# A pair's two heads on the row halves of the array in the scans' scores, and a later unpacking of the inverted triangles

## The chip, the core and the metric

The kernel runs on one core of a Trainium2 chip. The metric is the device time of one execution in microseconds. Three runs of the kernel before took 4954.92 to 4966.74 us, with a median of 4965.7 us.

## What is computed

Two layers over 2048 latent tokens and 256 context tokens of width 1024. The second layer is attention of a differential kind and isn't touched. The first is an RWKV-7 mixer: for each of 16 heads of size 64 a state S of 64 x 64 is carried over the tokens, once forward and once backward.

```python
def step(S, inp):
    r_t, w_t, k_t, v_t, kk_t, a_t = inp
    sa = jnp.einsum("bhvk,bhk->bhv", S, kk_t)
    S = (S * w_t[:, :, None, :]
         - sa[..., None] * (kk_t * a_t)[:, :, None, :]
         + v_t[..., None] * k_t[:, :, None, :])
    return S, jnp.einsum("bhvk,bhk->bhv", S, r_t)
...
oc_f, sc_f = scan_direction(con, 0, s0, False)
oc_b, sc_b = scan_direction(con, 1, s0, True)
ol_f, _ = scan_direction(lat, 0, sc_f, False)
ol_b, _ = scan_direction(lat, 1, sc_b, True)
```

The kernel works in chunks of 64 tokens. Within a chunk the recurrence becomes matrix products of 64 x 64 for each head (the scores), a triangular inverse for each head, and a short chain that takes the state from chunk to chunk.

## The kernel before, in words

`block` runs `setup`, `phase1` (projections and streams, written to DRAM), `phase2` (the scans), `readout`, `project1`, `attention` and `finish`. The change touches `phase2` alone, which lies at about 1150 to 2270 us of the profiled span.

**The loop.** There are 36 chunks in each direction, taken alternately: step q works on direction q % 2. The loop runs over q from -9 to 71. In one pass it makes the scores of step s = q + 9 and the chain of step q, so scores lie nine steps ahead. The order of work on TensorE, VectorE, ScalarE and GpSimd is the order in which the program lists it (`in_order`). SP, which issues all DMAs, isn't in that list: its order is made by the framework's planner.

**One pass.** Each kind of work is a generator that is advanced piece by piece. `step(c)` comes first (L796: the two products with RX, 32 records each for LA and LB), then the pieces in the order of `MAIN`, where u is `unpack`, b is `turned`, g is `scores`, j is `join` and c is `chain`:

```python
MAIN = "ubgjugbcgujgc"
```

So a pass has three slots for u (positions 0, 4 and 9), two for b (four transposes of BK each, L773, copied to KB by ScalarE, L774), four for g, two more for the chain (L804, and then L813 and L818 with the updates of RX and the store of o, L827) and two for j (U by VectorE at L742, and L749 with its copies).

**Scores.** A pair p holds two heads, A on partitions 0 to 63 (LO) and B on 64 to 127 (HI). For head A the tiles are BA and LA, loaded on LO and zero on HI; for head B they are BB and LB, loaded on HI and zero on LO. Each matmul contracts over all 128 rows. The four pieces of g are A with pairs 0 to 3, A with 4 to 7, B with 0 to 3 and B with 4 to 7. A piece takes one PSUM bank of a pool of three (`sc`, shared with `turned`), issues four f32 matmuls of 128 x 128 x 128 (L680, two records each), and then ScalarE copies parts to A32 (L687, twice) and E (L690), and VectorE makes the two masked products, one into the other half of L (L691) and one into Pb (L692).

**Loads.** `load(s)` issues BA, LA, BB and LB (L666, 256 KB each). BA and BB have two buffers, LA and LB ten. The zeros of the other halves are written once by GpSimd (L839).

**Inversion.** When four steps of scores are there (s % 4 == 3, so q % 4 == 2), VectorE transposes A32 to N (L699, L700) at the end of the pass, and GpSimd runs 30 rank-1 steps on it (L701 to L710). Four steps later, in the pass with q % 4 == 2, `unpack` makes four transposes on VectorE: two to Tt (L715, L717) and two to Dg (L719, L721). Three fall in that pass, one at each slot for u, and the fourth at slot 0 of the next. That next pass also has `join_rows` right after `step(c)` (L733, it reads Tt) and `join(0)` (it reads Dg).

Of the kernel before, what the change touches and what calls it, by code (L numbers as in the profile page):

```python
# [11 lines left out]
F32 = mybir.dt.float32  # L12
# [609 lines left out]
def phase2(k):  # L622

    nc, tc, S = k.nc, k.tc, k.S
    ident = k.ident
    LO, HI = slice(0, 64), slice(64, 128)
    LEAD = 9
    with ExitStack() as st:
        pool = lambda name, bufs, **kw: st.enter_context(tc.tile_pool(name=name, bufs=bufs, **kw))
        c0 = pool("p2z", 1)  # L630
# [16 lines left out]
        f2 = lambda ap: ap.rearrange("p a b -> p (a b)")  # L647
        ji = "p i j -> p j i"


        wide = [128, NPAIR, 2, 64]
        space = lambda pool, name: pool.tile(wide, F32, name=name)
        BAs, BBs, LAs, LBs = ([space(c0, f"{name}0")] for name in ("BA", "BB", "LA", "LB"))
        for i in range(1, LEAD + 1):
            for ring, name in ((LAs, "LA"), (LBs, "LB"), (BAs, "BA"), (BBs, "BB")):
                if i == 1 or ring is LAs or ring is LBs:
                    ring.append(space(c2[i - 3] if i > 2 else cb if i == 1 and name[0] == "L" else ca, f"{name}{i}"))
        Dg = c2[-1].tile([128, 32, 32], F32, name="Dg")
        U = c2[-1].tile([128, 32, 64], F32, name="U")

        def load(s):
            d, n = s % 2, ORDER[s % 2][s // 2]
            LA, LB = LAs[s % (LEAD + 1)], LBs[s % (LEAD + 1)]
            BA, BB = BAs[s % 2], BBs[s % 2]
            for t, nm, rows in ((BA, "bk", LO), (LA, "qr", LO), (BB, "bk", HI), (LB, "qr", HI)):
                nc.sync.dma_start(out=t[rows], in_=S[nm][d, n, rows])  # L666
            return LA, LB, BA, BB

        def scores(d, par, loaded, A32, E, Pb):

            LA, LB, BA, BB = loaded
            yield LA, LB, Pb
            br, kr = brow[d], krow[d]
            for ab in range(2):
                L, B = ((LA, BA), (LB, BB))[ab]
                for q in range(2):
                    ps = sc.tile([128, 4, 2, 64], F32, name="scps")
                    for j in range(4):
                        p = 4 * q + j
                        nc.tensor.matmul(f2(ps[:, j]), f2(B[:, p]), f2(L[:, p]), start=(j == 0), stop=True,  # L680
                                         skip_group_check=True)
                    prs = slice(4 * q, 4 * q + 4)
                    h0 = 8 * ab + 4 * q
                    c0 = 16 * par + h0
                    for blk in range(2):
                        r = slice(br.start + 32 * blk, br.start + 32 * blk + 32)
                        nc.scalar.copy(A32[r, :, c0:c0 + 4].rearrange("p t c -> p c t"),  # L687
                                       ps[r, :, d, 32 * blk:32 * blk + 32])
                    e, ec = (slice(0, 32), slice(32, 64)) if d == 0 else (slice(96, 128), slice(0, 32))
                    nc.scalar.copy(E[e, c0:c0 + 4, :], ps[e, :, d, ec])  # L690
                    nc.vector.tensor_tensor(L[krow[ab], prs], ps[kr], bcast(mk[kr, d], 1, 4), op=ALU.mult)  # L691
                    nc.vector.tensor_tensor(Pb[br, h0:h0 + 4], ps[br, :, 1 - d], bcast(mk[br, d, 1 - d], 1, 4),  # L692
                                            op=ALU.mult)
                    yield
# [138 lines left out]
        none = inv = iter(())  # L833
        step = lambda g: next(g, None)
        loaded[0], loaded[1] = load(0), load(1)
        for i in range(LEAD + 1):
            for t, rows in ((BAs, HI), (LAs, HI), (BBs, LO), (LBs, LO)):
                if i < len(t):
                    nc.gpsimd.memset(t[i][rows], 0.0)  # L839
            if i == 0:  # L840
                mk = causal_masks(k, ca)
        RX = []
        for d in range(2):
            RX.append(new_rx(0, d))
# [18 lines left out]
                yield from modulation(k, layer, lo, hi, 2, space, {lo // 4: bank()}, lambda: space()[0:2, :512], bank)  # L863

        at = (nq - LEAD) % (LEAD + 1)
        done = itertools.cycle((BAs[0], BBs[0], LAs[at], LBs[at]))
        free = lambda: next(done).rearrange("p a b c -> p (a b c)")
        mods = [none, none]
        if k.mod:
# [2 lines left out]
        with in_order(k, mybir.EngineType.PE, mybir.EngineType.DVE, mybir.EngineType.Activation, mybir.EngineType.Pool):  # L872
            for q in range(-LEAD, nq):
                s = q + LEAD
                b = c = g = u = j = none
                if 0 <= q + 1 < nq:
                    keys[q + 1] = load_keys(q + 1)
                if q >= 0:
                    KB = kp.tile(wide, F32, name="KB")
                    b = turned(keys.pop(q), KB)  # L880
                    c = chain(q // 2, q % 2, q // 2 % 2, prep.pop(q), KB)
                step(c)
                more = q >= -2 and q - q % 4 + 4 < nq
                if more and q % 4 == 3:
                    for par in range(2):
                        join_rows(tiles[q // 4 + 1][1], par)
                    j, late = join(0), join(1)
                if more and q % 4 == 2:
                    unp = unpack(tiles[q // 4 + 1][2])
                    u = none if q < 0 else unp  # L890
                if more and q % 4 == 3:
                    u = unp
                if q >= 0 and q % 4 == 0:
                    j = late
                if s < nq:
                    if s % 4 == 0:
                        tiles[s // 4] = [ip.tile([128, 32, 32], F32, name="A32", bufs=1),
                                         ip.tile([128, 32, 32], F32, name="E", bufs=2), None]
                    A32, E, _ = tiles[s // 4]
                    if s % 2 == 0:  # L900
                        Pb = pb.tile([128, 16, 64], F32, name="Pb")
                    g = scores(s % 2, s // 2 % 2, loaded.pop(s), A32, E, Pb)
                    prep[s] = step(g)
                who = {"u": u, "j": j, "b": b, "c": c, "g": g}
                for at, name in enumerate(MAIN):
                    step(who[name])
                    if name == "g":
                        step(inv)
                    if s >= nq and at in TAIL:
                        step(mods[1])  # L910
                    if -5 <= q < 0 and at in FILL:
                        step(mods[0])
                if q == -2:
                    for who in (inv, inv, unp, unp, unp):
                        step(who)
                if 1 <= s < nq - 1:
                    loaded[s + 1] = load(s + 1)
                if s < nq and s % 4 == 3:
                    inv = invert(A32, nc.vector if s < 4 else nc.gpsimd)
                    tiles[s // 4][2] = step(inv)  # L920
                    if s >= 4:
                        for _ in inv:
                            pass
# [774 lines left out]
```

## Time and profile before

| | |
|---|---|
| median of three runs | 4965.7 us |
| profiled execution, time | 4953.41 us |
| its span | 4951.7 us |
| TensorE busy | 4658.2 us (94%) |
| VectorE busy | 3706.7 us (75%) |
| ScalarE busy | 2700.0 us (55%) |
| GpSimd busy | 1457.7 us (29%) |
| granted clock, mean | 0.972 |

The shares are means over stages with different limits, so they say little of the scan. The rows that matter are those of the stretch from 1300 to 2100 us, in which the scan runs in a steady state. TensorE's records overlap, so that the start of one group to the start of the next tells more than the busy time. An entry such as `[0.55 <-POOL N L710]` is idle time of that engine just before the instruction, and what ended it.

### The profile page before, as it was taken

Reading aid. Unit: us, or ns where it says so; the run is one execution under the profiler, and the core shown is the slowest. Engines: PE = TensorE matmul, PEld = TensorE weight load, DVE = VectorE, ACT = ScalarE, POOL = GpSimd, SP = SyncE. Lnnn points to the kernel's source line nnn. Section 1 sums busy time; section 2 is a strip of 40 time slices with the busy share of each in tenths; the row PEclk is TensorE's granted clock in tenths of the full one; section 3 lists DMA queues with packets and bytes.
Section 4 is the critical chain, followed back from the end, with each engine's and each line's share of the span. In section 5 each row is a group of like instructions: output and inputs, shape, how many; then the busy total and the mean of one; then the engine's idle time right before and its main releaser. Section 6 shows DMA issues by size and latency. Waiting matters only on the chain.

```text
span 4951.7 us, 100950 instructions
## 1 busy us (share of the span) xinstructions
PE 4658.2 (94%) x40786; PEld 4184.8 (85%) x40786; DVE 3706.7 (75%) x5806; ACT 2700.0 (55%) x4908; POOL 1457.7 (29%) x1806
## 2 busy tenths in 40 slices
PE   7999999997998889888989999989999999999999
PEld 5999999995888888876768888879888888898887
DVE  6888887887877777866768258238989989989843
ACT  4655655554666666655541221227777777777730
POOL 1222112112566565551312022022223323323300
PEclk8999999998999998989999999989999999999999
DMA  4565565557666676668853332230011011010042
GB/s 165 170 185 159 176 187 165 162 165 208 151 163 165 166 177 155 168 182 284 265 173 99 115 115 86 94 105 19 11 46 36 14 42 36 28 29 18 10 158 94
DMA packets 624787, 612.13 MB, mean 124 GB/s; under 512 B 31622, under 2 KB 529721, under 8 KB 623297
## 3 DMA queue, kind: packets, MB, share of 16 engines
q1 hardware_dynamic: 621841, 601.99, 42.1%
q8 instruction: 323, 5.29, 0.5%
q10 hardware_dynamic: 2480, 3.67, 0.2%
q14 instruction: 143, 1.17, 0.1%
HBM read 405.79 MB, written 199.77 MB: 122 GB/s over the span
## 4 chain that ended last, share of the span: by engine, by line
PE 62%; DVE 14%; issue 11%; DMA 5%; ACT 5%; POOL 2%; SPq 0%; ACTq 0%; POOLq 0%; DVEq 0%
PE mmps L939 18%; PE mmps L363 9%; PE pv L1462 8%; PE tps L1455 4%; PE sc L1416 4%; PE sc L1417 3%; PE xops L818 3%; PE scps L680 3%; DVE p L1419 3%; PE xops L796 3%; DVE p L1440 2%; DMA RS<-s_v 2%; PE chps L813 1%; PE tps L1365 1%; DVE U L742 1%
## 5 line engine op out<-in xcount | busy, mean ns | idle before, releaser
L1430 ACT ACTIVATE p<-p,m 128x2304 f32<-128x2304 f32 x256 | 568.8, 2222 | 201.6 <-DVE p L1419 199.4
L1462 PE MATMUL pv<-v,at 128*128 128x128 f32 x4608 | 626.1, 277 | 6.2 <-ACT at L1457 4.4
L1462 PEld LDWEIGHTS pv<-v,at 128*128 128x128 f32 x4608 | 564.3, 191 | 16.0 <-ACT at L1457 12.8
L1416 PE MATMUL sc<-ks,qh 128*128 128x512 f32 (+1 forms) x1280 | 520.1, 406 | 15.2 <-DVE p L1419 15.1
L1417 PE MATMUL sc<-ks,ql 128*128 128x512 f32 (+1 forms) x1280 | 463.9, 372 | 0.3 <-POOL ql L1397 0.3
L363 PE MATMUL mmps<-hH,wH 128*128 128x386 f32 x1632 | 429.5, 343 | 17.1 <-DVE sg L581 12.0
L1457 ACT COPY at<-tps 128x512 f32<-128x512 f32 (+1 forms) x640 | 345.3, 540 | 177.6 <-PE tps L1455 173.6
L363 PE MATMUL mmps<-hL,wH 128*128 128x386 f32 x1632 | 427.2, 342 | 8.4 <-DVE hL L92 8.4
L1440 DVE SCALAR_TENSOR_TENSOR p<-p,r,p 128x1152 f32<-128x1152 f32 x256 | 427.4, 1670 | 4.5
L939 PE MATMUL mmps<-wH,hH 128*128 128x512 f32 x1088 | 424.6, 390 | 3.1 <-ACT hH L91 3.1
L363 PE MATMUL mmps<-hH,wL 128*128 128x386 f32 x1632 | 425.0, 341 | 0.3 <-DVE nm_ss L197 0.3
L939 PE MATMUL mmps<-wH,hL 128*128 128x512 f32 x1088 | 424.0, 390 | 0.7 <-DVE hL L92 0.7
L939 PE MATMUL mmps<-wL,hH 128*128 128x512 f32 x1088 | 424.2, 390 | 0.0
L1419 DVE TENSOR_SCALAR_CACHE_REDUCE p<-sc,m 128x1280 f32<-128x1280 f32 x256 | 395.5, 1545 | 17.1 <-PE sc L1417 1.2
L1397 POOL TENSOR_TENSOR ql<-qt,qh 128x256 fp32r<-128x256 f32 x128 | 112.2, 877 | 977.8 <-ACT qt L1396 916.5
L1455 PE MATMUL tps<-ident,p 128*128 128x128 f32 x2304 | 361.5, 275 | 10.1 <-ACT qt L1396 5.2
L1419 DVE TENSOR_SCALAR_CACHE_REDUCE p<-sc 128x1024 f32<-128x1024 f32 x256 | 311.5, 1217 | 56.7 <-PE sc L1417 55.6
L1455 PEld LDWEIGHTS tps<-ident,p 128*128 128x128 f32 x2304 | 273.2, 141 | 60.6 <-ACT at L1457 10.9
L363 PEld LDWEIGHTS mmps<-hH,wH 128*128 128x128 f32 x1632 | 297.7, 191 | 21.1 <-DVE sg L581 15.5
L363 PEld LDWEIGHTS mmps<-hL,wH 128*128 128x128 f32 x1632 | 300.2, 190 | 10.4 <-DVE hL L92 9.2
L363 PEld LDWEIGHTS mmps<-hH,wL 128*128 128x128 f32 x1632 | 301.2, 190 | 0.8 <-DVE nm_ss L197 0.8
L707 POOL TENSOR_TENSOR N<-N,rank 128x30 f32<-128x30 f32 (+14 forms) x510 | 280.2, 549 | 40.0
(313 smaller groups left out, 10655.8 us busy)
## 6 DMA issues: line engine op xcount, KB each, us to landing
wr<-in_rw_in_dram SPq DMA_DIRECT2D x102, 512.0 KB
s_qr<-QR SPq DMA_DIRECT2D x48, 768.0 KB
BK<-s_bk SPq DMA_DIRECT2D x72, 512.0 KB
s_bk<-BK SPq DMA_DIRECT2D x47, 768.0 KB
wraw<-in_da_in_dram SPq DMA_DIRECT2D x64, 512.0 KB
BA<-s_bk SPq DMA_DIRECT2D x72, 256.0 KB
LA<-s_qr SPq DMA_DIRECT2D x72, 256.0 KB
BB<-s_bk SPq DMA_DIRECT2D x72, 256.0 KB
```

The costliest lines, as they stand in the source:

```text
L363: nc.tensor.matmul(a[:, :b1 - b0], wt[:, kt, :], ht[:, kt, b0:b1], start=(kt == 0 and wt is wH and ht is hH), stop=(kt == KT - 1 and last))
L680: nc.tensor.matmul(f2(ps[:, j]), f2(B[:, p]), f2(L[:, p]), start=(j == 0), stop=True, skip_group_check=True)
L707: eng.tensor_tensor(N[:, m + 1:32, 0:m], N[:, m + 1:32, 0:m], t, op=ALU.subtract)
L939: k.nc.tensor.matmul(ps, s(kt), m(kt), start=(kt == 0 and s is sH and m is mH), stop=(kt == KT - 1 and last))
L1416: nc.tensor.matmul(s[:, b0 - g0:b1 - g0], qh[:, cs], ks, start=True, stop=False)
L1417: nc.tensor.matmul(s[:, b0 - g0:b1 - g0], ql[:, cs], ks, start=False, stop=True)
L1419: nc.vector.tensor_scalar(tiles[n][c][:, g0:g1], s[:, :g1 - g0], -1.0, m, op0=ALU.mult, op1=ALU.min, accum_out=least)
L1430: nc.scalar.activation(P, P, AF.Exp, bias=m, scale=-1.0, accum_out=z)
L1440: nc.vector.scalar_tensor_tensor(P0[:, b0:b1], P1[:, b0:b1], r, P0[:, b0:b1], op0=ALU.mult, op1=ALU.add)
L1455: nc.tensor.transpose(ps[:, c - b0:c - b0 + 128], P0[:, c:c + 128], k.ident)
L1457: (eng.copy if eng is nc.scalar else eng.tensor_copy)(at[b][:, :b1 - b0], ps[:, :b1 - b0])
L1462: nc.tensor.matmul(acc, at[b][:, c - b0:c - b0 + 128], H.v[:, c // 128], start=(c == 0), stop=(c == T - 128))
```

## The change

BA and BB are replaced by one tile B with two buffers, loaded by one DMA of 512 KB for both halves. The score matmuls contract over 64 rows: head A on rows LO of B and LA, head B on rows HI of B and LB. For four pairs at a time both heads' matmuls are issued in turn (A, B, A, B, ...) into two PSUM banks that are taken together. Of the four pieces of g the first and the third now hold eight matmuls each, and the second and fourth hold none; what ScalarE and VectorE do after them is the same for each bank, in the order A and B of pairs 0 to 3, then A and B of pairs 4 to 7. The zeros are no longer written. The first two transposes of `unpack` stand at slots 4 and 9 of the pass with q % 4 == 2, and the other two both at slot 0 of the next pass.

```diff
@@ phase2
-        BAs, BBs, LAs, LBs = ([space(c0, f"{name}0")] for name in ("BA", "BB", "LA", "LB"))
+        LAs, LBs = ([space(c0, f"{name}0")] for name in ("LA", "LB"))
...
+        Bs = [space(c0, "B0"), space(ca, "B1")]
...
             LA, LB = LAs[s % (LEAD + 1)], LBs[s % (LEAD + 1)]
-            BA, BB = BAs[s % 2], BBs[s % 2]
-            for t, nm, rows in ((BA, "bk", LO), (LA, "qr", LO), (BB, "bk", HI), (LB, "qr", HI)):
-                nc.sync.dma_start(out=t[rows], in_=S[nm][d, n, rows])
-            return LA, LB, BA, BB
+            B = Bs[s % 2]
+            nc.sync.dma_start(out=B, in_=S["bk"][d, n])
+            for t, rows in ((LA, LO), (LB, HI)):
+                nc.sync.dma_start(out=t[rows], in_=S["qr"][d, n, rows])
+            return LA, LB, B
...
-            for ab in range(2):
-                L, B = ((LA, BA), (LB, BB))[ab]
-                for q in range(2):
-                    ps = sc.tile([128, 4, 2, 64], F32, name="scps")
-                    for j in range(4):
-                        p = 4 * q + j
-                        nc.tensor.matmul(f2(ps[:, j]), f2(B[:, p]), f2(L[:, p]), start=(j == 0), stop=True,
-                                         skip_group_check=True)
+            for q in range(2):
+                both = [sc.tile([128, 4, 2, 64], F32, name="scps") for _ in range(2)]
+                for j in range(4):
+                    p = 4 * q + j
+                    for ps, L, rows in zip(both, (LA, LB), (LO, HI)):
+                        nc.tensor.matmul(f2(ps[:, j]), f2(B[rows, p]), f2(L[rows, p]), start=(j == 0), stop=True,
+                                         skip_group_check=True)
+                for ab in range(2):
+                    ps, L = both[ab], (LA, LB)[ab]
...
-        for i in range(LEAD + 1):
-            for t, rows in ((BAs, HI), (LAs, HI), (BBs, LO), (LBs, LO)):
-                if i < len(t):
-                    nc.gpsimd.memset(t[i][rows], 0.0)
-            if i == 0:
-                mk = causal_masks(k, ca)
+        mk = causal_masks(k, ca)
...
                 for at, name in enumerate(MAIN):
-                    step(who[name])
+                    if name != "u" or at or q % 4 != 2:
+                        step(who[name])
+                    if name == "u" and not at and q % 4 == 3:
+                        step(u)
```

## Rows read from the trace of the kernel before

**Rows 1.** Stretch 1300:2100: busy us of PE, PEld, DVE, ACT, POOL; clock, DMA, GB/s.
```profile
1300.00:2100.00 800.00, 721.64 (x14583) 676.07 (x14585) 622.29 (x862) 522.32 (x1224) 472.92 (x868) 0.95 0.68 166
```

**Rows 2.** Waits, 1300 to 2100 us: engine, line, releaser, us, times, longest.
```profile
POOL N L701 <- DVE N L700: 265.5, 14, 27.5
...
PE chps L813 <- DMA RS<-s_v: 18.8, 21, 2.0
...
PE scps L680 <- DMA LB<-s_qr: 11.5, 13, 1.9
DVE Tt L715 <- POOL N L710: 10.8, 8, 2.1
PEld chps L804 <- issue: 9.4, 54, 0.5
```

**Rows 3.** GpSimd's timeline: start, us, line, tiles; an inversion's first and last.
```profile
1757.88 1.26 POOL L701 TENSOR_SCALAR_AFFINE_SELECT N<-N 128x1024 f32<-128x1024 f32 x1 [17.29 <-DVE N L700]
...
1796.73 0.15 POOL L710 MEMSET N<- 128x32 f32 x1
```

**Rows 4.** VectorE's timeline: U in a step 0, then steps 2 and 3.
```profile
1718.45 2.99 DVE L742 TENSOR_SCALAR U<-Dg 32x512 f32<-32x512 f32 x4
...
1740.63 2.11 DVE L715 STREAM_TRANSPOSE Tt<-N 32x1024 f32<-32x1024 f32 x1 [0.55 <-POOL N L710]
1743.17 0.68 DVE L691 TENSOR_TENSOR LA<-scps,causal 64x512 f32<-64x512 f32 x1 [0.44 <-ACT E L690]
...
1744.33 1.98 DVE L717 STREAM_TRANSPOSE Tt<-N 32x1024 f32<-32x1024 f32 x1
...
1748.65 1.96 DVE L719 STREAM_TRANSPOSE Dg<-N 64x1024 f32<-64x1024 f32 x1
...
1751.78 0.68 DVE L824 TENSOR_TENSOR RX<-chps,RX 64x512 f32<-64x512 f32 x1
...
1760.52 1.88 DVE L742 TENSOR_SCALAR U<-Dg 32x512 f32<-32x512 f32 x4
```

**Rows 5.** TensorE's timeline: steps 0 and 1, and the starts of later ones.
```profile
1712.78 1.15 PE L796 MATMUL xops<-RX,LA 128*64 128x64 f32 x32
...
1715.29 1.95 PE L680 MATMUL scps<-LA,BA 128*128 128x128 f32 x16
...
1718.68 1.16 PE L680 MATMUL scps<-LB,BB 128*128 128x128 f32 x8
...
1722.95 1.15 PE L813 MATMUL chps<-RS,KB 128*64 128x64 f32 x32
1724.04 2.08 PE L818 MATMUL xops<-RS,Pb 64*64 64x64 f32 x32
1726.04 1.15 PE L796 MATMUL xops<-RX,LA 128*64 128x64 f32 x32
...
1738.66 1.15 PE L796 MATMUL xops<-RX,LA 128*64 128x64 f32 x32
...
1767.24 1.15 PE L796 MATMUL xops<-RX,LA 128*64 128x64 f32 x32
```

**Rows 6.** ScalarE's timeline: the second KB copy of the step 0 above.
```profile
1718.19 0.59 ACT L774 COPY KB<-scps 128x512 f32<-128x512 f32 x1
```

**Rows 7.** The memsets of L839: one of its forms, and who waited for them.
```profile
L839 POOL MEMSET LA<- x10: 946/946/953, 810.5 to 1176.3; 64x1024 f32 x10
...
  PEld scps L680: 3.9, 3
```

**Rows 8.** SP's timeline, a step 2 and the begin of the next step.
```profile
1739.38 0.46 SPq L827 DMA_DIRECT2D s_o<-RS  x1
1739.93 1.19 SPq L666 DMA_DIRECT2D LB<-s_qr  x1
...
1744.28 0.54 SPq L666 DMA_DIRECT2D LA<-s_qr  x1
...
1751.38 0.59 SPq L666 DMA_DIRECT2D BB<-s_bk  x1
```

More of the change, by code (lines that the diff above doesn't have):

```diff
@@ L652, in phase2 @@
         space = lambda pool, name: pool.tile(wide, F32, name=name)
-        BAs, BBs, LAs, LBs = ([space(c0, f"{name}0")] for name in ("BA", "BB", "LA", "LB"))
+        LAs, LBs = ([space(c0, f"{name}0")] for name in ("LA", "LB"))
         for i in range(1, LEAD + 1):
-            for ring, name in ((LAs, "LA"), (LBs, "LB"), (BAs, "BA"), (BBs, "BB")):
-                if i == 1 or ring is LAs or ring is LBs:
-                    ring.append(space(c2[i - 3] if i > 2 else cb if i == 1 and name[0] == "L" else ca, f"{name}{i}"))
+            for ring, name in ((LAs, "LA"), (LBs, "LB")):
+                ring.append(space(c2[i - 3] if i > 2 else cb if i == 1 else ca, f"{name}{i}"))
+        Bs = [space(c0, "B0"), space(ca, "B1")]
         Dg = c2[-1].tile([128, 32, 32], F32, name="Dg")
@@ L663, in load @@
             LA, LB = LAs[s % (LEAD + 1)], LBs[s % (LEAD + 1)]
-            BA, BB = BAs[s % 2], BBs[s % 2]
-            for t, nm, rows in ((BA, "bk", LO), (LA, "qr", LO), (BB, "bk", HI), (LB, "qr", HI)):
-                nc.sync.dma_start(out=t[rows], in_=S[nm][d, n, rows])
-            return LA, LB, BA, BB
+            B = Bs[s % 2]
[3 more added lines that the diff above has]
+            return LA, LB, B
         def scores(d, par, loaded, A32, E, Pb):
-            LA, LB, BA, BB = loaded
+            LA, LB, B = loaded
             yield LA, LB, Pb
             br, kr = brow[d], krow[d]
-            for ab in range(2):
-                L, B = ((LA, BA), (LB, BB))[ab]
-                for q in range(2):
-                    ps = sc.tile([128, 4, 2, 64], F32, name="scps")
-                    for j in range(4):
-                        p = 4 * q + j
-                        nc.tensor.matmul(f2(ps[:, j]), f2(B[:, p]), f2(L[:, p]), start=(j == 0), stop=True,
+            for q in range(2):
[4 more added lines that the diff above has]
+                        nc.tensor.matmul(f2(ps[:, j]), f2(B[rows, p]), f2(L[rows, p]), start=(j == 0), stop=True,
                                          skip_group_check=True)
+                for ab in range(2):
+                    ps, L = both[ab], (LA, LB)[ab]
                     prs = slice(4 * q, 4 * q + 4)
@@ L865, in phase2 @@
         at = (nq - LEAD) % (LEAD + 1)
-        done = itertools.cycle((BAs[0], BBs[0], LAs[at], LBs[at]))
+        done = itertools.cycle((Bs[0], Bs[1], LAs[at], LBs[at]))
         free = lambda: next(done).rearrange("p a b c -> p (a b c)")
```

## The prediction

> **What bounds the kernel now.** I read the busy time of each engine over the steady scan first, then who waited for whom, then the engines' timelines over one whole period. Over 800 us of the scan TensorE is busy 721.6 us, VectorE 622.3 us and GpSimd 472.9 us, with a granted clock of 0.95 and the DMA engines busy 0.68 [rows 1]. The reader is to see that no engine is full: TensorE leads, and yet 10% of it is idle. So something goes round in a circle. The work repeats every four steps (a step is one pass of the loop over q, and starts on TensorE with L796); 14 inversions lie in the 800 us, 57.1 us each [rows 2]. I call the steps 0 to 3 by q modulo 4.
>
> The first circle is the inversion. GpSimd starts at 1757.88 and has N ready at 1796.88, 39.0 us [rows 3]. VectorE then unpacks it and, in the same run of work, makes the next N: from the first unpacking transpose at 1740.63 [rows 4] to the end of L700, which lets the next inversion start at 1757.88, 17.3 us [rows 3]. Neither can start before the other ends, so a period can't be under 39.0 + 17.3 = 56.3 us, close to the 57.1 us seen. In 8 of 14 periods the first transpose waits for GpSimd, 10.8 us in all [rows 2]. A shorter score block alone can therefore bring next to nothing here.
>
> The second circle is the step itself. Steps 0 and 1 start at 1712.78 and 1726.04, step 2 at 1738.66, the next step 0 at 1767.24: 13.26, 12.62 and, for steps 2 and 3 together, 28.58 us [rows 5]. In steps 0 and 1 VectorE has much less to do, and TensorE's list sets the pace, with waits for the V rows (L813 on RS, 18.8 us in 800) and for LB (11.5 us) [rows 2]. In steps 2 and 3 VectorE runs nearly without a gap from its transposes to U [rows 4].
>
> **The score blocks.** The matmul count stays at 16 a step (32 records, since one f32 matmul leaves two). Before, 16 records on the full array took 1.95 us, 0.11 us each once the last one's latency is taken off [rows 5]. What a pair on two row halves costs the trace doesn't show. The nearest rows are L796, which alternates between the column halves, 32 records in 1.15 us, and L818, which stays in one quarter, 32 in 2.08 us, with the same 64 columns [rows 5]. So two halves ran at the same time at the price of one. The bounds for a new block of 16 records are 0.9 us (side by side) and 1.8 us (one after the other). I take 0.9 us: the column halves are the nearest thing, and the two heads write to different PSUM banks here. A step's scores then fall from 3.6 to 1.8 us on TensorE.
>
> The Trainium skill, page "TensorE: Matmul & The Clock Gate", section "Measured speedup vs the span model", gives four row tiles 3.07 times the speed, not 4. By that a block would be an estimated 1.2 us and about half of the gain below would be left; no run here shows it yet.
>
> **What takes its place.** Both heads of four pairs are now issued together, so head B's bank is filled earlier and the second block needs two free banks of three at once. In step 1 the first block starts 2.5 us after the step's start [rows 5] and ends at 3.4 us. ScalarE's copies and VectorE's two products (1.16 us, from 1743.17 to 1744.33 [rows 4]) free head A's bank at 5.75 us, and the second KB copy frees the third bank at 6.0 us (1718.19 + 0.59 against 1712.78 [rows 5, 6]). So the second block starts at 6.1 and ends at 7.0 us, where TensorE alone would have been there at 4.9 us. RS is copied by 7.4 us, L813 and L818 take 3.1 us (1722.95 to 1726.04 [rows 5]): step 1 lasts 10.6 us instead of 12.6 us. Step 0 also has the join: U is written after head A's products, at 8.1 us, then 1.1 us of L749 and 3.1 us: 12.3 us instead of 13.3 us.
>
> **The unpacking, moved.** The first two transposes leave slots 0 and 4 of step 2 for slots 4 and 9, and the third moves to step 3. They issue no DMA; what is queued behind them is VectorE's own list. In step 2 the first now starts after head A's products, at 5.75 us, where it stood at 2.0 us (1740.63 against 1738.66 [rows 4, 5]). From there: 2.1, three pairs of products at 1.16, 2.0 for the second, and 6.0 for the RX updates and both N transposes (1751.78 to 1757.88 [rows 3, 4]) make 13.6 us. The circle with GpSimd shrinks from 56.3 to 39.0 + 13.6 + 0.1 = 52.7 us: that is what the move is worth, since it is no longer last. What is last next is VectorE: N ends at 19.4 us of step 2, two Dg transposes take 3.9 us (two of 1.96), head A's products 1.16 us, U 2.3 us (between the 1.88 and 2.99 us of [rows 4]), then L749 and L813 and L818 4.2 us: 31.0 us for steps 2 and 3, 2.4 us more than before.
>
> **Sum.** 31.0 + 12.3 + 10.6 = 53.9 us a period against the 56.3 us of the circle now: -2.4 us; I take -2.1 us, since U may also take the longer time. Of the scan's 72 steps 63 have scores beside the chain, some 15.5 periods: -32 us. The 24 memsets that go lie on GpSimd, 0.95 us each [rows 7], beside the filling of the pipeline; TensorE waited 3.9 us for them [rows 7], of which I count 2 (bounds 0 and 4). The waits for RS and LB stay between nothing and the 30 us that they are now; counted at no change. Together -34 us: the profiled execution's 4953.4 us (span 4951.7 us) would be 4919 us. The median of the runs, 4965.7 us, lies 12 us over the profiled one, so the median would be **4932 us**. About 0.3% (15 us) is what a measurement of this kernel can tell from no change.
>
> **Rivals.** *LB behind the store.* The loads of the next step stand on SP in an order that the planner makes. Now BA and LA go ahead of the store of o and LB behind it, BB in every second step too: o at 1739.38, LB at 1739.93, LA at 1744.28, BB behind the next o at 1751.38 [rows 8]. The store waits for the end of the step, so LB is issued 1.3 us into the step that uses it. That is harmless now, as LB is used by the third block, 5.9 us in (1718.68 against 1712.78 [rows 5]); 13 of 56 steps waited for it [rows 2], so it lands at about 5.4 us. The changed scores need LB in the first block at 2.5 us, and everything on TensorE queues behind it. For it: three loads in place of four keep the bytes, and LB is still the last. Against: one issue fewer on SP, and a later end of the step gives LB time to get ahead. Decides: whether LB's issue stands behind L827. Each late step costs 2.9 us, step 3 none, as VectorE hides it. If the order alternates, as BB does now, 2 late steps a period: 5.8 - 2.1 = 3.7 us, +57 us, 5023 us; if in every step, 8.7 - 2.1 = 6.6 us, +102 us, 5068 us.
>
> *No halves at once.* The block stays at 1.8 us: step 1 would be 12.0, step 0 13.2, steps 2 and 3 1.2 us longer, 3.5 us in all, +1.4 us net a period: +22 us, 4988 us.
>
> *The wrong bank.* If the planner gives the second block the bank of head B and not that of KB, it waits for the last products of the first: with U or a transpose between, 2 to 3 us in steps 0, 2 and 3, 6.6 us a period, net 4.5: +70 us, 5036 us.
>
> *Shape changes eat it.* TensorE stands idle 0.17 us when L804 follows the transposes (9.4 us, 54 times [rows 2]); the other changes of tile shape show no gap. Up to four more a step, in the two steps that TensorE sets, are 0.17 x 4 x 2 = 1.4 us a period, +21 us: 4953 us, no change. The Trainium skill, page "TensorEngine Tiling (Array Packing)", section "Key Properties", says that a change of tiling mode drains TensorE; the 0.17 us row agrees, the other changes don't, which is why this has a small chance only.
>
> **How the numbers follow.** Forecast 0.46 (own range 4900 to 4952 us); shape changes 0.13; LB late in every second step 0.16, in every step 0.11; no halves 0.07; wrong bank 0.07. Faster by over 0.3%: most of the forecast and a little of the shape changes, 0.45. Within: 0.15. Slower: 0.40. The range that leaves out some 2 in 10 runs from 4900 us to 5040 us, up to the wrong bank and the alternating order; LB late in every step lies outside.
>
> **What would show it.** In the profile after: 16 records of L680 in about 1 us, starts of LA and LB records in pairs; LB issued ahead of L827; the first transpose no longer waiting for GpSimd; N to N about 54 us; step 1 near 10.6 us. A wait of the first block for LB in most steps would make the prediction wrong in sign, a block of 1.8 us in size, and a wait of the second block of over 2 us would point to the banks.

## The result: 0.65% slower, with TensorE at the lower clock for over a quarter of the scan

The changed kernel took 4989.6 us (median of five runs, 4985.15 to 4999.47) against 4965.7 us for the kernel before (five runs): 1.0065 times the time, with a 95% interval of 1.0049 to 1.0081, some 30 us (the ratio is taken over the runs; the two medians lie 23.9 us apart). Its profiled execution took 4985.15 us, with a span of 4983.0 us, 31.3 us more than the span before. Cut at four places, the two spans differ like this:

| part of the span | before, us | after, us | difference |
|---|---|---|---|
| up to the scan's first step (first record of L796, now L797) | 1253.0 | 1251.5 | -1.5 |
| the scan (to the end of the last L818, now L819) | 1015.5 | 1029.0 | +13.5 |
| from there to the readout's first product (L939, now L938) | 7.5 | 28.9 | +21.4 |
| the rest | 2675.6 | 2673.5 | -2.1 |

So in these two executions there are two losses: one in the scan, where a gain of 32 us was forecast, and one just behind it, of which the prediction says nothing. The size of the first is the less sure one, since the profiled execution before lies 12.3 us under its kernel's median and the one after 4.4 us under. The forecast gain is missing either way.

**The scan.** The window of [rows 1], now of the kernel after (columns as there):

```profile
1300.00:2100.00 800.00, 687.65 (x14322) 623.97 (x14316) 616.96 (x844) 510.16 (x1201) 465.61 (x861) 0.85 0.57 163
```

TensorE is busy for 34 us less, as it should be with less matmul time, but the granted clock is 0.85 in place of 0.95. The granted clock has two levels in these traces, 1.0 and 0.5 (2.4 and 1.2 GHz), so 0.85 means that TensorE ran at the lower one for about 30% of the time. Taken step by step over one period (the step starts are those of L797; these windows are step 0, 1, 2 and 3, same columns):

```profile
1672.40:1685.60 13.20, 12.10 (x267) 11.02 (x268) 8.22 (x14) 9.13 (x22) 11.79 (x19) 0.91 0.67 181
1685.60:1696.80 11.20, 10.05 (x202) 8.99 (x203) 7.33 (x13) 8.38 (x20) 9.23 (x21) 1.00 0.74 210
1696.80:1707.20 10.40, 9.61 (x203) 8.69 (x202) 8.48 (x13) 7.97 (x20) 0.00 (x0) 1.00 0.69 198
1707.20:1730.70 23.50, 19.18 (x395) 17.34 (x394) 21.24 (x26) 11.96 (x26) 12.53 (x24) 0.68 0.38 120
```

The reader is to see where the clock falls: in step 3 (0.68), with the end of the low stretch in the next step 0 (0.91). TensorE's waits in the 800 us say what it does in step 3 (columns as in [rows 2]):

```profile
POOL N L702 <- DVE N L701: 286.7, 14, 25.3
...
PE scps L679 <- ACT KB L775: 69.8, 55, 3.7
...
ACT A L688 <- DVE N L701: 34.7, 14, 3.0
...
PE scps L679 <- DVE Pb L693: 26.4, 14, 2.0
...
PE chps L750 <- DVE U L743: 6.9, 18, 0.5
```

The waits of [rows 2] for LB, for RS and of VectorE's L715 for GpSimd are gone. In their place the second score block waits for its two PSUM banks. The first wait, for the bank that ScalarE's KB copy frees, comes in every step (55 times). The kernel before had it too, but seldom:

```profile
PE scps L680 <- ACT KB L774: 21.7, 13, 2.6
```

The second wait, for the bank that head A's products free, comes once a period (14 times), in step 3. Here is TensorE's timeline of that step, from its second score block on (start, us, line, tiles, and the idle time just before with what ended it):

```profile
1715.98 1.15 PE L805 MATMUL chps<-X,U 128*64 128x64 f32 x32
1718.86 0.53 PE L679 MATMUL scps<-LA,B 64*128 64x128 f32 x2 [1.73 <-ACT KB L775]
1721.31 0.58 PE L679 MATMUL scps<-LB,B 64*128 64x128 f32 x1 [1.92 <-DVE Pb L693]
...
1723.31 1.92 PE L750 MATMUL chps<-U,Tt 32*32 32x32 f32 x64
1725.15 1.98 PE L814 MATMUL chps<-RS,KB 128*64 128x64 f32 x32
1727.06 3.67 PE L819 MATMUL xops<-RS,Pb 64*64 64x64 f32 x32
```

TensorE stands idle for 1.73 and 1.92 us with only a piece of a block between, and what follows runs at half speed: L814 and L819, which took 1.15 and 2.08 us in [rows 5], take 1.98 and 3.67 us. The step has two low stretches, each with a granted clock of 0.5. The long one, from 1719.2 to 1732.8, begins just behind the first wait, takes in the second and lasts into the next step 0. In it lies the end of step 3: from the start of L750 to the next step's start 7.35 us go by, in 13 of the 14 periods. A short one, from 1712.3 to 1715.8, lies ahead of both waits and holds the first score block, whose records take 0.42 us (0.27 at full clock) and follow at 0.21:

```profile
1713.67 0.42 PE L679 MATMUL scps<-LA,B 64*128 64x128 f32 x1
1713.68 0.42 PE L679 MATMUL scps<-LB,B 64*128 64x128 f32 x1
1713.89 0.42 PE L679 MATMUL scps<-LA,B 64*128 64x128 f32 x1
```

VectorE's and ScalarE's timelines show why the banks come late:

```profile
1713.04 1.24 DVE L700 STREAM_TRANSPOSE N<-A 64x1024 f32<-64x1024 f32 x1
1714.29 1.94 DVE L701 STREAM_TRANSPOSE N<-A 64x1024 f32<-64x1024 f32 x1
1716.26 2.01 DVE L720 STREAM_TRANSPOSE Dg<-N 64x1024 f32<-64x1024 f32 x1
1718.30 1.97 DVE L722 STREAM_TRANSPOSE Dg<-N 64x1024 f32<-64x1024 f32 x1
1720.16 0.66 DVE L692 TENSOR_TENSOR LA<-scps,causal 64x512 f32<-64x512 f32 x1
...
1721.18 2.26 DVE L743 TENSOR_SCALAR U<-Dg 32x512 f32<-32x512 f32 x4
```
```profile
1716.34 0.77 ACT L688 COPY A<-scps 32x128 f32<-32x128 f32 x2 [2.29 <-DVE N L701]
...
1718.24 0.57 ACT L775 COPY KB<-scps 128x512 f32<-128x512 f32 x1
```

VectorE makes the two N transposes and then, by the change, both Dg transposes, before it comes to head A's products at 1720.16. ScalarE can't copy the new scores into A32 before N has been read from it, since A32 has one buffer, and the KB copy queues behind that wait. So both banks wait for VectorE's list.

The Trainium skill, page "TensorE: Matmul & The Clock Gate", section "A second HAM failure mode: psum-queue depth-cycling", tells of a kernel whose TensorE idles briefly between groups of matmuls as it goes round its PSUM banks, and whose clock swings between its two levels for that. This trace agrees in part: in 13 of 14 periods the long low stretch begins 10.7 to 12.9 us into step 3, during or just behind the wait for KB's bank (1.73 us above). The short stretch has no such wait ahead of it. Whether the waits are the cause is tested below.

**Behind the scan.** TensorE's waits around the scan's end, of the kernel before and then of the kernel after:

```profile
PE mmps L939 <- ACT yH L1006: 5.8, 2, 4.9
```
```profile
PE mmps L938 <- ACT yH L1005: 14.0, 1, 14.0
PE tps L999 <- DVE ob L992: 13.0, 1, 13.0
```

And one of the readout's loads of the o rows on SP, before and after:

```profile
2242.20 0.58 SPq L982 DMA_DIRECT2D ob<-s_o  x1
```
```profile
2280.92 0.43 SPq L981 DMA_DIRECT2D ob<-s_o  x1
```

Before, this load went out 26 us ahead of the scan's end (2268.5); after, only when the scan was over (2280.5), and TensorE waited for what is made of the rows.

### The profile page after: what moved, and what is told of

The parts are those of the page before. It is cut to its first block, busy times and chain, and to the rows that moved or that the text cites. A ratio compares the mean times of both kernels' runs of the same rounds, so it can differ in the third digit from the quotient of the medians.

```text
span 4983.0 us, 100957 instructions
## 1 busy us (share of the span) xinstructions
PE 4621.5 (93%) x40786; PEld 4128.0 (83%) x40786; DVE 3714.6 (75%) x5806; ACT 2696.6 (54%) x4908; POOL 1430.7 (29%) x1782
## 3 DMA queue, kind: packets, MB, share of 16 engines
q10 hardware_dynamic: 2480, 3.67, 0.3%
## 4 chain that ended last, share of the span: by engine, by line
PE 63%; DVE 14%; issue 13%; ACT 5%; POOL 2%; DMA 2%; SPq 0%; ACTq 0%; POOLq 0%; DVEq 0%
PE mmps L938 19%; PE pv L1461 8%; PE mmps L363 7%; PE tps L1454 4%; PE sc L1415 4%; PE sc L1416 4%; PE xops L819 4%; PE xops L797 3%; PE scps L679 3%; DVE p L1418 2%; PE chps L814 2%; DVE p L1439 2%; PE scps L774 1%; PE chps L750 1%; PE tps L1364 1%
## 5 line engine op out<-in xcount | busy, mean ns | idle before, releaser
L363 PE MATMUL mmps<-hH,wH 128*128 128x386 f32 x1632 | 429.5, 343 | 16.6 <-DVE sg L581 12.1
L938 PE MATMUL mmps<-wH,hH 128*128 128x512 f32 x1088 | 424.7, 390 | 3.1 <-ACT hH L91 3.1
L938 PE MATMUL mmps<-wH,hL 128*128 128x512 f32 x1088 | 424.0, 390 | 0.8 <-DVE hL L92 0.8
L938 PE MATMUL mmps<-wL,hH 128*128 128x512 f32 x1088 | 424.3, 390 | 0.0
L1454 PE MATMUL tps<-ident,p 128*128 128x128 f32 x2304 | 361.6, 275 | 10.4 <-ACT qt L1395 5.4
L1418 DVE TENSOR_SCALAR_CACHE_REDUCE p<-sc 128x1024 f32<-128x1024 f32 x256 | 311.6, 1217 | 56.6 <-PE sc L1416 55.5
L363 PEld LDWEIGHTS mmps<-hL,wH 128*128 128x128 f32 x1632 | 300.3, 190 | 10.4 <-DVE hL L92 9.2
L688 ACT COPY A<-scps 32x128 f32<-32x128 f32 x576 | 214.8, 373 | 170.1 <-PE scps L679 117.3
```

Of the source, the lines that this page charges most:

```text
L363: nc.tensor.matmul(a[:, :b1 - b0], wt[:, kt, :], ht[:, kt, b0:b1], start=(kt == 0 and wt is wH and ht is hH), stop=(kt == KT - 1 and last))
L938: k.nc.tensor.matmul(ps, s(kt), m(kt), start=(kt == 0 and s is sH and m is mH), stop=(kt == KT - 1 and last))
L1418: nc.vector.tensor_scalar(tiles[n][c][:, g0:g1], s[:, :g1 - g0], -1.0, m, op0=ALU.mult, op1=ALU.min, accum_out=least)
L1454: nc.tensor.transpose(ps[:, c - b0:c - b0 + 128], P0[:, c:c + 128], k.ident)
```

## The experiments

Each row: the ratio to the kernel before with its 95% interval; from the profiled execution, the mean of the 14 periods from the fifth step on (starts of L797) and how much of a period was at half clock; the scan; and the gap behind it.

| kernel | ratio | period, us | of it at half clock | scan | gap |
|---|---|---|---|---|---|
| before | 1 | 57.9 | 5.6 | 1015.5 | 7.5 |
| changed | 1.0065 (1.0049 to 1.0081) | 58.7 | 16.5 | 1029.0 | 28.9 |
| changed, second profile | 1.0061 (1.0040 to 1.0081) | 59.3 | 17.8 | 1032.4 | 29.1 |
| e1 move undone | 1.0058 (1.0044 to 1.0072) | 58.1 | 16.6 | 1013.4 | 29.1 |
| e2 move alone | 1.0108 (1.0090 to 1.0126) | 61.0 | 9.8 | 1065.2 | 7.5 |
| e3 places | 1.0059 (1.0044 to 1.0073) | 59.5 | 18.0 | 1041.8 | 5.8 |
| e4 block repeated | 1.0031 (1.0012 to 1.0050) | 56.8 | 8.6 | 999.2 | 29.8 |
| e5 halves apart | 1.0014 (1.0003 to 1.0026) | 58.2 | 17.7 | 1018.0 | 29.3 |
| places and block repeated | 0.9996 (0.9982 to 1.0010) | 56.4 | 7.8 | 1001.8 | 7.8 |
| e7 join last | 0.9926 (0.9913 to 0.9938) | 56.1 | 11.5 | 980.9 | 5.8 |
| new order | 0.9818 (0.9804 to 0.9831) | 52.5 | 4.7 | 926.5 | 5.8 |
| f1 new order, one A32 | 0.9865 (0.9844 to 0.9887) | 53.9 | 7.8 | 954.0 | 5.8 |
| f2 before, new order | 0.9956 (0.9938 to 0.9973) | 56.8 | 4.1 | 989.5 | 7.5 |
| f3 new order, early unpacking | 0.9923 (0.9904 to 0.9942) | 55.6 | 9.8 | 978.3 | 5.8 |

A profiled execution can lie some 12 us off its kernel's median: those of the kernel before, of e1 and of the places with the block repeated lie 12 us under it, that of e4 9 us under and that of f1 8 us over. So scans that differ by 20 us or less don't rank two kernels; the ratios do.

**The changed kernel again.** No edit.

> The changed kernel, unedited, beside the others: a second profiled execution of it. All theories expect 4980 to 5000 us, a scan of 1020 to 1040 us, 270 to 300 us of it at half clock, and a gap of about 29 us to the readout's first product. What it tells: how much the number of the long periods (62 to 63 us, where the half clock reaches into steps 0 and 1) varies from one execution to the next; a few us of the scan's time up or down is not to be explained by an edit.

It took 4993.3 us. Four of its 14 periods lasted 62 to 64 us, against two in the first profile: those where the low clock reaches far into step 0. A scan can so differ by several us with no edit. The point at which the scores begin also moves, from 1153.3 to 1165.2 us of the span, and the first step follows 98.2 and 98.4 us behind it (98.3 in the kernel before). So the start of the scan tells nothing of the memsets that were removed.

**The two parts, each alone.** First the changed kernel with the early unpacking:

```diff
-                    if name != "u" or at or q % 4 != 2:
-                        step(who[name])
-                    if name == "u" and not at and q % 4 == 3:
-                        step(u)
+                    step(who[name])
```

> The changed kernel with the unpacking put back to the slots it had before; scores on row halves stay. Theory G (gap and clock): in the changed kernel TensorE stands idle in step 3 behind VectorE's N and Dg transposes, and the granted clock falls to 0.5 for about 13.7 us in every period. With the unpacking early again VectorE has done a third of it before the score products, so the idle time in step 3 is shorter, and less time is spent at half clock than the 283 us of the changed kernel's scan: period 55.5 to 57 us (again bounded by the circle of GpSimd's 39.0 and VectorE's 17 us), 15 to 40 us below the changed kernel, about 4950 to 4975 us. Rival S (the row halves alone bring the slow step, the move is innocent): step 3 stays at 23 us, the half-clock time at about 280 us, and the circle is longer besides: 4990 us or more.

Then the kernel before, with the opposite edit:

> The kernel before with the later unpacking only; scores on the full array with zero rows. Theory G: the later unpacking pushes VectorE's work into step 3, step 3 gets about 2 us longer and TensorE idles there; with four score blocks of 2 us TensorE has more to do in that time, so the clock falls less than in the changed kernel: about +30 us against the kernel before, 4995 us. Rival S (move innocent): the circle with GpSimd is 3.7 us shorter, and the time is that of the kernel before or up to 30 us less.

Undoing the move brought no measurable time (4987.6 us). Step 3 fell to 19.3 us on average, but step 2 rose to 12.6 us, with 11 to 19 us in the six periods where its unpacking waited for GpSimd, and half clock took as much of a period as in the changed kernel (16.6 us). So theory G was right on the shorter step 3 and wrong on what it brings; rival S was near on the half clock and the time and wrong on step 3. The half clock came with the row halves, then, and not with the move; and of the 29 us by which this kernel is slower than the kernel before, the gap behind the scan makes 21.6. The move alone cost 1.08%, some 53 us (5009.7 us), more than the 30 expected: a period grew from 57.9 to 61.0 us. In its 800 us TensorE waited 17 us longer for VectorE's U (25.9 us, 8.8 before) and 10 us longer for RS and LB, together 1.9 us a period, and 4.2 us more of a period was at half clock. So the late unpacking as such is a loss in this order of work. With both parts together the loss is smaller than with the move alone: the two are not a sum.

**The places.** The changed kernel with two unused tiles where the dropped ones stood, which also take their turn as space for the second layer's modulation:

```diff
-        Bs = [space(c0, "B0"), space(ca, "B1")]
+        Bs, pads = [space(c0, "B0")], [space(c0, "pad0")]
...
+            if i == 1:
+                Bs.append(space(ca, "B1"))
+                pads.append(space(ca, "pad1"))
...
-        done = itertools.cycle((Bs[0], Bs[1], LAs[at], LBs[at]))
+        done = itertools.cycle((Bs[0], pads[0], LAs[at], LBs[at]))
```

> The changed kernel with two unused tiles of the same size in the places where BA, BB stood, so that all later tiles lie where they lay before, and with the same four tiles given back to the projection behind the scans. The scan's work is unchanged. Theory P: the 20.5 us that the changed kernel loses between the scan's last step and the readout's first product come from tiles that lie elsewhere, so that the loads of the o rows and of the readout's weight are issued only after the scan's end: that gap goes from 31.7 back to about 11 us, the time by 20 us to about 4969 us, and the scan's steps stay at 58 us a period. Rival: the gap comes from the scan's new order of loads; then the gap stays at about 31 us and the time at 4989 us.

The gap fell from 28.9 to 5.8 us, and TensorE's wait for the first product's input to this:

```profile
PE mmps L945 <- ACT yH L1012: 3.1, 1, 3.1
```

So the gap comes from where the tiles lie and from the modulation's space, which this edit changed together; they were not tried one by one. But the time hardly fell (4988.6 us), where theory P had 4969. In this profile the last steps give back 6 to 10 us of it: from the 61st step to the end the scan took 150.6 us, against 144.6 and 140.4 in the two profiles of the changed kernel. That doesn't hold for all kernels with these places (e7: 138.9 us), and where the rest of the 23 us went isn't shown.

**TensorE kept at work.** The changed kernel, with the first score block's matmuls five times in place of once in step 3:

```diff
-                for j in range(4):
+                for j in range(4 * (again if q == 0 else 1)):
+                    j = j % 4
...
-                    g = scores(s % 2, s // 2 % 2, loaded.pop(s), A32, E, Pb)
+                    g = scores(s % 2, s // 2 % 2, loaded.pop(s), A32, E, Pb, 5 if q % 4 == 3 and q > 0 else 1)
```

> The changed kernel, but in each step 3 (q modulo 4 is 3) TensorE repeats the first score block's matmuls four times more (4 x about 0.9 us, into the same banks with the same values), as work for its idle time. Theory C (the clock): the idle time in step 3 makes the granted clock fall to 0.5 for about 13.7 us, and that stretches step 3 and the next step 0 by 4 to 5 us a period. With the idle time filled the clock stays near 1.0 there, the period falls from 58 to 53.5 to 55 us, and the time by 45 to 70 us, to about 4920 to 4945 us. Rival V (VectorE's path sets step 3, the clock matters little): the period stays at 58 us and the time at 4989 us. If the added 3.6 us were themselves on the path, the period would be 60 us or more, and the time about 5030 us.

More work made it faster: 4973.3 us, 0.3% less than the changed kernel, which the intervals only just separate, and the scan went from 1029 to 999 us. The clock over 1300 to 2100 us was 0.93. The gain is below the 45 us expected, since in nine of the 14 periods the clock still fell in step 3, only later, after the wait for head A's products. In these nine, 7.1 to 7.9 us went by from the join's matmuls to the end of step 3, and steps 2 and 3 took 32.7 to 33.6 us. In the other five it was 4.4 to 4.7 us, close to the 4.2 us of the sum, and steps 2 and 3 took 30.3 to 30.9 us. And one period of this kernel ran at full clock from end to end (steps 0 to 3, columns as above):

```profile
1663.40:1675.60 12.20, 10.96 (x266) 9.89 (x265) 10.37 (x17) 9.15 (x22) 10.95 (x17) 1.00 0.66 196
1675.60:1686.20 10.60, 9.76 (x204) 8.84 (x202) 7.67 (x13) 8.36 (x20) 9.42 (x16) 1.00 0.59 168
1686.20:1696.60 10.40, 9.60 (x202) 8.68 (x201) 8.68 (x13) 8.00 (x20) 4.50 (x12) 1.00 0.91 264
1696.60:1716.50 19.90, 17.34 (x458) 15.88 (x457) 18.88 (x23) 11.91 (x26) 9.27 (x20) 1.00 0.45 136
```

That is 53.1 us, where the prediction had 53.9: 12.2 (12.3) + 10.6 (10.6) + 30.3 (31.0). The same steps took 58.3 us in the changed kernel above. So the half clock cost about 5 us a period. This is the run that shows what the half clock costs, since the edit adds nothing to VectorE's list.

With the places as well:

> Two edits together: the tiles in the places that they had before (unused tiles where BA and BB stood) and the first score block's matmuls repeated four times more in step 3. If the two causes are separate, the gap from the scan's end to the readout's first product is 6 to 8 us in place of 29 and the scan is some 30 us shorter than the changed kernel's 1029 us: 40 to 50 us less than the changed kernel, about 4940 to 4950 us, below the kernel before. If the loads that come earlier into the scan's last steps slow these by as much as the gap wins (the kernel with the places alone had the shorter gap and no shorter median), the time is that of the repeated block alone, about 4973 us.

4962.9 us, 0.35% less than with the block repeated alone: the gap (7.8 us) and the scan (1001.8 us) came as expected, and the time is that of the kernel before, not below it as expected. Against e3, which lacks only the repeated block, it is 0.63% less (1.0059 and 0.9996), clear of the intervals. Here too the scan's end took longer, 156.8 us from the 61st step against 145.4 in e4.

**The halves apart.** The changed kernel, one head's four matmuls after the other's:

```diff
-                for j in range(4):
-                    p = 4 * q + j
-                    for ps, L, rows in zip(both, (LA, LB), (LO, HI)):
+                for ps, L, rows in zip(both, (LA, LB), (LO, HI)):
+                    for j in range(4):
+                        p = 4 * q + j
```

> The changed kernel with one thing undone: the two heads' matmuls are issued one head after the other (four of A, then four of B), so that the row halves don't work at the same time and a block of 16 records should take 1.8 us in place of 0.95. Everything else stays. Theory C (the clock eats the gain): at full clock step 1 would be 12.0 us and step 0 13.2 us, some 4 us a period more than the 53.1 us that the changed kernel needs where its clock doesn't fall; but TensorE is idle for less of the time, so the clock falls less often: less than 200 us of the scan at half clock in place of 287, a period of 57 to 59 us and a time within 20 us of the changed kernel, 4970 to 5010 us. Rival V (the clock falls as before, since the idle times in step 3 come from VectorE's list, which is unchanged): half clock for some 280 us and 3 to 4 us a period more, about 62 us, +55 us, 5045 us.

Undoing the very speed-up of the blocks made the kernel faster, 4969.8 us. Part of TensorE's timeline in a step 1, the two blocks' begins and what follows them, first of this kernel:

```profile
1685.75 0.82 PE L679 MATMUL scps<-LA,B 64*128 64x128 f32 x5
...
1687.39 0.66 PE L774 MATMUL scps<-ident,BK 128*128 128x128 f32 x4
1687.98 1.15 PE L805 MATMUL chps<-X,U 128*64 128x64 f32 x32
1689.12 0.79 PE L679 MATMUL scps<-LA,B 64*128 64x128 f32 x5
```

and of the changed one, with the first block's pairs:

```profile
1688.75 0.37 PE L679 MATMUL scps<-LA,B 64*128 64x128 f32 x1
1688.76 0.37 PE L679 MATMUL scps<-LB,B 64*128 64x128 f32 x1
1688.96 0.27 PE L679 MATMUL scps<-LA,B 64*128 64x128 f32 x1
1688.97 0.27 PE L679 MATMUL scps<-LB,B 64*128 64x128 f32 x1
...
1689.84 0.66 PE L774 MATMUL scps<-ident,BK 128*128 128x128 f32 x4
1690.43 1.15 PE L805 MATMUL chps<-X,U 128*64 128x64 f32 x32
1692.43 0.37 PE L679 MATMUL scps<-LA,B 64*128 64x128 f32 x1 [0.85 <-ACT KB L775]
```

From a block's start to the next matmul's start it takes 1.64 us apart (1685.75 to 1687.39) and 1.09 us together (1688.75 to the transposes at 1689.84). Apart isn't quite apart: the last three records of A lie among the first of B, and the block takes less than the 1.8 us expected. But together, TensorE then stands 0.85 us before the second block, waiting for KB's bank, and apart it doesn't. So steps 1 and 2 took 10.8 and 10.7 us in place of 10.6 and 10.4: the halves at once were worth 0.2 to 0.3 us a step here, not the 1.4 us that I had priced. The half clock did not become rarer (17.7 us a period; under 200 us of the scan were expected), so neither theory's account holds in full. TensorE's waits for the two score banks fell from 96 to 12 us in 800, it was busy for 766.6 us of them, and yet the granted clock was 0.85 again. In 11 of 14 periods it now fell 5 to 7 us into step 3, around an idle time of 0.5 to 1.9 us at or next to the products of the join's rows (L734). So the waits for banks are not all that lowers the clock, and whether it matters for it that the score matmuls now use half of the rows was not tested by itself (the repeated matmuls of e4 use half of them too, and the clock rose). What did change is that no period lasted longer than 60.7 us; why this kernel is, by the ratios, some 0.5% faster than the changed one stays open.

**TensorE's list in step 3.** The places of before, and the join's matmuls behind the chain's last part:

```diff
-MAIN = "ubgjugbcgujgc"
+MAIN = "ubgjugbcgugcj"
```

> The changed kernel with the tiles in the places of before, and one change of order in every step: the join's products (which wait for VectorE's U) are listed behind the chain's last part (KB and Pb products) in place of ahead of it. Theory O (TensorE's list order makes the idle time): in step 3 TensorE waits for U with the chain's 3.1 us of ready work queued behind the join; with that work first the wait of L750 for U goes, step 3 is 1 to 3 us shorter and step 0 about 1 us, and the clock falls less: period 53 to 56 us, 30 to 70 us below the changed kernel with the places alone, 4920 to 4960 us. Rival V (VectorE's own list ends the step, as the next step's scores wait for its products): the period stays at 58 us and the time at 4985 us.

4927.0 us, within what theory O gave. The wait of L750 for U is gone and step 0 took 12.5 us on average where e3 had 14.6. Step 3 itself, 22.6 against 23.2 us, gained little: its two waits for banks are still there. The next kernel attacks these, with A32 in two buffers (in the place of one unused tile) and head A's products ahead of Dg in step 3:

```diff
-                for at, name in enumerate(MAIN):
+                for at, name in enumerate("bguujgbcgugcj" if more and q % 4 == 3 else MAIN):
                     if name != "u" or at or q % 4 != 2:
                         step(who[name])
-                    if name == "u" and not at and q % 4 == 3:
-                        step(u)
...
-                        tiles[s // 4] = [ip.tile([128, 32, 32], F32, name="A32", bufs=1),
+                        tiles[s // 4] = [ip.tile([128, 32, 32], F32, name="A32", bufs=2),
```

> As the kernel with the join last, and besides: in step 3 VectorE makes head A's first two products before the two Dg transposes in place of after them, and A32 has two buffers, so that ScalarE needn't wait for the N transposes before it copies the next scores. Theory O: both waits of TensorE's second score block in step 3 (for KB's bank, held up because ScalarE stood waiting for N; and for head A's bank, held up by the Dg transposes) go as well; step 3 falls to 16 to 18 us, the clock stays near 1.0, and the circle with GpSimd (39.0 + 13.7 us) is last: period 52.7 to 54 us, 4900 to 4935 us. Rival V: VectorE's work of steps 2 and 3 sets the period whatever the order, 57 us or more, 4970 us or more.

4872.7 us, 1.8% below the kernel before and, by the ratios, 2.5% below the changed one. Step 3 took 18.2 us, the period 52.5 us, which is the circle that I had worked out (39.0 + 13.6 + 0.1 = 52.7). VectorE now waits for GpSimd in 13 of the periods, a sign that the circle is last; the waits for banks are shorter:

```profile
PE scps L681 <- ACT KB L777: 43.7, 59, 0.9
...
DVE Tt L718 <- POOL N L713: 17.4, 13, 2.4
```

**The change's parts, with the order mended.** The same with one A32:

> The kernel with the new order of step 3 (head A's products ahead of the Dg transposes, the join last), but with one A32 buffer as in the changed kernel, so that ScalarE again waits for the N transposes before it copies the first scores, and KB's copy queues behind it. If the order alone removes TensorE's long waits: step 3 at 17 to 19 us, a period of 52.5 to 54 us, 4870 to 4895 us. If ScalarE's wait holds the second score block as it did (3 us of idle time on TensorE in step 3), the clock falls again for 10 us or more a period: 54.5 to 56.5 us, 4905 to 4930 us.

The same order in the kernel before, with the late unpacking and one A32:

> The kernel before (scores on the full array with zero rows) with the later unpacking and the new order of step 3, one A32 buffer (a second doesn't fit beside BA and BB). If the two-fold matmul time of the scores is not what bounds the scan once the order is mended: step 0 12.3 us, step 1 12.6, steps 2 and 3 about 29, a period of 53 to 54.5 us, 4890 to 4925 us. If TensorE's time for the scores counts in every step (0.9 us a block, two blocks a step, four steps: 7 us): 57 us or more, 4955 us or more.

And the new order with the early unpacking:

> The fastest kernel so far (new order, join last, two A32 buffers, row halves) with the unpacking put back to the early slots of step 2. My prediction's circle: GpSimd's 39.0 us and VectorE's 17.3 us from the first unpacking transpose to N can't overlap, so the period is 56.3 us again, some 55 us more than with the late unpacking: 4920 to 4935 us. Rival: the circle was never last, and the period stays at 52.5 to 54 us, 4870 to 4895 us.

These gave 4895.7, 4943.4 and 4922.0 us. By the ratios, the second A32 buffer is worth 0.47% (0.9865 to 0.9818), the row halves 0.91% (0.9956 to 0.9865, both with one A32) and the late unpacking 1.05% (0.9923 to 0.9818). f1's period (53.9 us) and f3's time are as expected, and f1's time lies a little above its first range; f2 lies between its two. With the early unpacking VectorE waits for GpSimd for 59.2 us in place of 17.4, and the inversions start 55.5 to 55.8 us apart in every period, as the circle has it in this run (38.8 us on GpSimd and 16.8 on VectorE):

```profile
DVE Tt L718 <- POOL N L713: 59.2, 14, 6.9
```

So once step 3's order is mended, each part of the change brings some 45 to 52 us.

## Why the prediction was wrong

It forecast 4932 us, faster. The time was 4989.6 us, slower: within the range, but by a way that none of the rivals described. That the rival without halves stands at 4988 us is a coincidence, since the halves did work at the same time. Point by point:

- **The block at the price of one half.** Right in kind: both halves work at the same time. From its start to the next matmul's start a block takes 1.09 us, where it took 1.79 us before (medians at full clock) and 0.9 was forecast. The records of the pairs keep the pace of 0.11 us, but some 0.1 us is added behind the first pair and behind the last. The 1.2 us estimated from the Trainium skill (page "TensorE: Matmul & The Clock Gate", section "Measured speedup vs the span model") lie a little nearer to it.
- **Step 1, and the second block's bank.** Right: 10.6 us, and the second block waits for KB's copy.
- **The circle.** Right: from the first unpacking transpose (1702.59) to the next inversion (1716.31) are 13.7 us, 13.6 forecast, and the transpose no longer waits for GpSimd. What it was set against was less right: the period of [rows 5] lasts 54.5 us, under the 56.3 us said to be the least, and the mean of the kernel before is 57.9 us.
- **Steps 2 and 3 at 31.0, step 0 at 12.3.** Here it failed. They took 33.8 and 13.6 us (medians). VectorE's terms came out: in the period shown N ends 19.4 us after the start of step 2 and U 26.6 us after it, 19.4 and 26.8 forecast. The step that failed is the term behind them, L749, L813 and L818 at 4.2 us: it measured 7.35 us, as TensorE was at its lower clock there, and the first 2 to 5 us of step 0 were so too. The term comes from rows at full clock, out of a period that had no half clock at all, where the kernel before has 5.6 us of it in the mean. The mean clock of 0.95 was read in [rows 1] without asking in which step it is lost, and what would happen to it if TensorE got less work in the very step where it already waits for VectorE. At full clock the sum holds: 53.1 us in e4, 53.9 forecast.
- **The unpacking moved.** It was costed as 2.4 us more in steps 2 and 3 against a shorter circle. That VectorE's Dg transposes then stand ahead of the products that free TensorE's banks is in the sum as VectorE's time, but not as TensorE's idle time. Alone it cost some 53 us.
- **The memsets, -2 us.** Nothing to be seen: 98.2 us from the first scores to the first step, 98.3 before.
- **What is missing.** 21.4 us behind the scan: two tiles fewer move the other tiles and the space for the modulation, and the readout's loads go out later; e3 undid both together, and the gap went. The prediction looked at no line outside of the scan but the memsets.
- **The rivals.** LB was not late: no wait for it is left. The changes of shape cost some 0.2 us a block, and step 1 came out as forecast all the same, since the second block waits for KB's bank in any case. The banks were the ones I had expected. "No halves" was overpriced: my sum had 1.4 us for step 1, and e5, where the halves hardly overlap, shows 0.2.

## What to carry to other kernels

Before taking matmul time away, look in which stretch TensorE already waits, and with which granted clock: time taken away there can lengthen the wait, and if the clock falls, it can cost as much as it gave. If a change loses, see what it has made last, and reorder that (here VectorE's products ahead of its transposes, ready matmuls ahead of waiting ones) before giving the change up. Dropping a tile can move the loads of a later stage, so read the stage behind as well.

## What the runs showed of the hardware

Matmuls that were pure repetition made the kernel 0.3% faster, and 0.6% with the tiles in the places of before, because TensorE's clock was at its upper level for longer (0.93 in place of 0.85 from 1300 to 2100 us). And two f32 matmuls on the two row halves, into two banks, start within 0.01 us of each other, and the pairs follow at 0.11 us, the pace of a single one.
